# Hybrid encoder layer: the second norm's per-row scale applied behind the MLP, its transposes taken by column half, and the step sizes' sums issued behind the gated attention

## Chip, cores and metric

One core of a Trainium2 chip runs the whole program. Times are device microseconds (us) of that core. Six engines appear below: PE (matrix products, with PEld for its weight loads), DVE, ACT and POOL (elementwise work), SP (issues most DMAs), and the DMA queues.

## What is computed

One encoder layer runs on two requests with the same weights: a prompt of 256 tokens and a sample of 512 tokens, 1024 features each.

```python
def rmsnorm(x, g):
    return x * lax.rsqrt(jnp.mean(x * x, axis=-1, keepdims=True) + EPS) * g

h = rmsnorm(x, norm1)
(gq, gk, gv, gg, glr, dq, dk, dvv, sz, sxbc, sdt) = jnp.split(h @ w_in, IN_OFFSETS, axis=-1)
o_gla  = gla_mixer(gq, gk, gv, gg, glr, ...)     # gated attention, 4 heads, forward and backward
o_diff = diff_mixer(dq, dk, dvv, ...)            # w = softmax 1 - lam * softmax 2, 4 heads
o_ssd  = ssd_mixer(sz, sxbc, sdt, ...)           # state space scan, 8 heads, forward and backward
x = x + jnp.concatenate([o_gla, o_diff, o_ssd], axis=-1) @ w_out
h = rmsnorm(x, norm2)                            # the second norm
x = x + jnp.square(jax.nn.relu(h @ w_mlp1)) @ w_mlp2

# in ssd_mixer: the step sizes and their running sums
dt_f = jax.nn.softplus(sdt[..., :8] + dtb_f)
la   = dt * -exp(alog);  acum = jnp.cumsum(la, axis=1)
```

## The kernel before

**Tiles.** The 768 tokens are six tiles of 128 rows: tiles 0 and 1 are the prompt, tiles 2 to 5 the sample. Every product is made of three passes in a reduced fp32 form, high part by high part and the two mixed ones (mm3, L96 to L100). So each operand is a pair: ACT writes the high part and DVE the rest. Weights go through load_unit (L137): a DMA of 512 KB on SP into wr (two buffers), an ACT cast to wh (L134) and a DVE subtraction to wl (L135). Three kinds of product are used: fm (features on the partitions, 384 token columns in the first projection, 256 or 512 in the MLP), tm (tokens on the partitions, 256 columns), and tp (tokens on the partitions, 512 columns, added to the residual rows xres).

**What sets the order.** The body is written stage after stage, and a framework's scheduler, which has a timing model of its own, merges the stages engine by engine: it takes whatever is ready by that model, earlier-written work and work in a high_priority block first. An engine runs its list strictly in that order, so an instruction that waits holds up all that is behind it on that engine.

**Stages.** First norm and transposes; the first projection's low-rank gate and step-size columns (glr, L234); ssd_dt (L503); gates of the gated attention (gla_gates, L263), whose cores run on DVE, POOL and short products (gla_core, L340); then projections for the other mixers, each interleaved with attention: diff_in (L753) makes queries, keys and values, diff_head (L786) scores sc, softmax pr and its transposed weights wT; SSD convolution and chunks (L566 to L750); then for the prompt W_out (tok_product, L891), second norm (norm2, L1148, which calls norm_transpose, L166) and MLP (mlp, L934), interleaved with the sample's attention and SSD; last the sample's W_out, second norm and MLP, which have no other stage beside them.

**Step sizes (ssd_dt, L503).** On 16 partitions of 768 columns: ACT Abs, Exp, Ln (L507 to L509), then ten DVE instructions with one scan over the tokens (dpre, L522). SP stores rows of the sums to DRAM as scr (L533, L534) and the chunk totals as scp (L535), and reads scp back on all partitions as ptb (L536). ACT makes the decays decs from ptb (L543). PE transposes the sums to tokens on partitions, ACT copies them out of PSUM (tms, L552 to L556) and makes ew from them (L558 to L563). decs, tms and ew are used by the SSD chunks and states.

**Second norm (norm_transpose, L166).** For each row tile: ACT squares and sums a row (L172), DVE makes mean square plus EPS (L158), POOL raises it to -0.5 (L159), DVE writes scaled rows xn (L177). PE transposes xn 128 x 128 into a PSUM tile xT (L184), ACT and DVE apply the feature's gain as they split xT into the pair h (L185, L186). For the sample this runs on two pairs of row tiles, since the last W_out product there goes row tile by row tile (by_tile, L906), and the first MLP block therefore uses two halves of 256 columns. For the prompt it runs once both row tiles are complete.

Of the kernel before, what the change touches and what calls it, by code (L numbers as in the profile page):

```python
# [19 lines left out]
P = 128  # L20
D = 1024
# [21 lines left out]
def hybrid_kernel(ctx, tc, io):  # L43
# [64 lines left out]
    pool.memset(ones, 1.0)  # L108
    nhalf = const.tile([P, 16], F32, name="nhalf")
# [51 lines left out]
    def rstd1(out, ss, scale):  # L161
        rstd_of(out, ss, 1, scale, small2)

    scaled = []

    def norm_transpose(xs, r0, tiles, hT, xn_of, ps_of, small, rstd, c0):  # L166

        xn = []
        for t in tiles:
            y = xn_of(xs[t])  # L170
            ss = small("ss", 1)
            sq = act.activation(y[2], xs[t], AF.Square, accum_out=ss)  # L172
            rs = small("rs", 1)
            rstd(rs, ss, 1.0 / D)
            for i in range(2):
                cs = slice(512 * i, 512 * i + 512)
                scaled[:] = [sq.ins, dve.tensor_scalar(y[i], xs[t][:, cs], rs, None, op0=ALU.mult).ins]  # L177
            xn.append(y)
        n = len(tiles) * P
        sl = slice(c0, c0 + n)  # L180
        for k in range(KT):
            ps = ps_of("xT")
            for i, y in enumerate(xn):
                nc.tensor.transpose(ps[:, i * P:(i + 1) * P], y[k // 4][:, (k % 4) * P:(k % 4 + 1) * P], ident)  # L184
            last = (act.activation(hT[k][0][:, sl], ps[:, :n], AF.Copy, scale=gains[:, r0 + k:r0 + k + 1]),  # L185
                    dve.scalar_tensor_tensor(hT[k][1][:, sl], ps[:, :n], gains[:, r0 + k:r0 + k + 1], rd(hT[k][0][:, sl]),  # L186
                                             op0=ALU.mult, op1=ALU.subtract))
        return last

    hT = [(hs_("hTh", F32R), hs_("hTl", F32R)) for _ in range(KT)]  # L190
    for tiles in ((0,), (1,), (2, 3), (4, 5)):
        normed = norm_transpose(xt, 0, tiles, hT, lambda x: (x[:, 0:512], x[:, 512:1024], junk), mx, small, rstd1, tiles[0] * P)
# [34 lines left out]
    zdt = s3("zdt")  # L227
# [79 lines left out]
    def gla_qk(hp):  # L307
# [195 lines left out]
    def ssd_dt():  # L503

        ps_ = slice(96, 112)
        z, t1, u, l = zdt[ps_], t3("dz")[ps_], t3("dt2")[ps_], t3("dl")[ps_]
# [8 lines left out]
        stk = t3("stk")  # L515
        pool.memset(stk, 0.0)
        dve.scalar_tensor_tensor(stk[0:16], z, 0.0, l, op0=ALU.max, op1=ALU.add)
        dtl = t3("dtl")[ps_]

        dve.tensor_scalar(dtl, stk[0:16], sdtc[0:16, 3:4], -128.0, op0=ALU.mult, op1=ALU.max)  # L520
        inc, exc = t3("dpre")[ps_], t3("dexc")[ps_]
        dve.tensor_tensor_scan(inc, resetm[ps_], dtl, 0.0, ALU.mult, ALU.add)  # L522
# [5 lines left out]
        stb = t3("stb")  # L528
# [6 lines left out]
        nc.sync.dma_start(out=scp, in_=v128(inc)[:, :, 127])  # L535

# [27 lines left out]
        return scr, decs, tms, ew  # L564
# [311 lines left out]


# [13 lines left out]
    def tok_product(op, n, wsrc, k0, tiles, done=None, by_tile=False, after=()):  # L891
# [4 lines left out]
        def product(ps, w, t, i, c):  # L896
            for k in range(4):
                mm3(ps, op(i + k, t), (w[0][:, k], w[1][:, k]), i + k == 0, i + k == n - 1)
            if i + 4 == n:
                cs = slice(c, c + 512)  # L900
                dve.tensor_tensor(xres[t][:, cs], ps, xres[t][:, cs], ALU.add)  # L901
                if done is not None:
                    done(t, c + 512)

        if by_tile:
            ws = [load(c, 0) for c in range(0, D, 512)]  # L906
# [317 lines left out]
```

## Time and profile before

| | us |
|---|---|
| three timed runs | 1166.26, 1168.5, 1172.04 |
| median | 1168.5 |
| the profiled execution | 1169.03 |
| its span in the trace | 1167.2 |
| around the span | 1.83 |

The mean granted clock of TensorE over the span is 0.976 of full speed. Below, the granted clock has two levels: 1.0 in a column PEclk stands for 2.4 GHz and 0.5 for 1.2 GHz. The trace comes from one execution; a group "xT<-ident,xn" means that the instruction writes the tile xT and reads ident and xn. A figure in square brackets is the idle time of the engine ahead of that instruction, with the instruction that ended it.

### The profile page before, as it was taken

The page shows a single profiled execution, that of the slowest core. Times are in us where ns is not written, and L with a number is a line of the kernel's source. Part 1 is how long each engine was busy: PE and PEld are TensorE (multiplying, and loading weights), DVE is VectorE, ACT ScalarE, POOL GpSimd, SP SyncE. Part 2 cuts the span into 40 slices and gives each one's busy share as a digit, 9 for nine tenths or more (in the row PEclk, how much of TensorE's full clock was granted, in tenths as well). Part 3 has the DMA queues.
Part 4 walks back from the last instruction along what each step waited for, and adds up shares of the span by engine and source line. Part 5 has one row for each costly group of instructions (what it writes and reads, how often), then busy time and mean ns, then how long its engine had stood idle before and what let it go on. Part 6 is the DMA issues. An engine that isn't in the chain of part 4 may idle for free.

```text
span 1167.2 us, 19741 instructions
## 1 busy us (share of the span) xinstructions
PE 1110.8 (95%) x7868; PEld 978.6 (84%) x7868; DVE 737.8 (63%) x1298; ACT 563.9 (48%) x1119; POOL 157.0 (13%) x208
## 2 busy tenths in 40 slices
PE   7989797999998999899989999999999999999998
PEld 6989697999998986788877897788887787787786
DVE  6559859563697668887677786846544534434443
ACT  7476666554377237756666573425231332322321
POOL 1002425310401360110100012200000000000000
PEclk9989798899999999899999999999999999999999
DMA  6312021171534355445543549522323323233231
GB/s 196 85 40 74 4 64 38 41 240 39 162 96 127 111 160 167 126 144 177 195 144 120 187 145 305 200 92 73 108 72 108 101 80 108 77 104 99 82 109 72
DMA packets 118642, 136.41 MB, mean 117 GB/s; under 512 B 8936, under 2 KB 86790, under 8 KB 118550
## 3 DMA queue, kind: packets, MB, share of 16 engines
q1 hardware_dynamic: 118517, 135.14, 36.6%
q8 instruction: 62, 1.02, 0.3%
q14 instruction: 31, 0.25, 0.1%
q10 hardware_dynamic: 32, 0.01, 0.0%
HBM read 121.44 MB, written 13.68 MB: 116 GB/s over the span
## 4 chain that ended last, share of the span: by engine, by line
PE 61%; DVE 16%; DMA 11%; ACT 6%; issue 3%; POOL 2%; SPq 0%; DVEq 0%; ACTq 0%; POOLq 0%
PE tp L98 7%; DMA wr<-in_w_mlp 7%; PE tp L99 7%; PE tp L100 7%; PE fm L98 6%; PE fm L100 6%; PE fm L99 6%; PE tm L100 5%; PE tm L99 5%; PE tm L98 5%; DVE wl L135 4%; ACT wh L134 2%; DMA er<-scr 1%; DVE d L428 1%; DVE eq L433 1%
## 5 line engine op out<-in xcount | busy, mean ns | idle before, releaser
L134 ACT CAST wh<-wr 128x1024 fp32r<-128x1024 f32 x186 | 189.2, 1048 | 236.5 <-PE tp L100 129.2
L135 DVE TENSOR_TENSOR wl<-wr,wh 128x1024 fp32r<-128x1024 f32 x186 | 224.2, 1229 | 93.4 <-ACT wh L134 92.8
L100 PE MATMUL tm<-wh,hTl 128*128 128x256 f32 x576 | 168.7, 293 | 0.0
L98 PE MATMUL tm<-wh,hTh 128*128 128x256 f32 x576 | 166.8, 290 | 0.5 <-ACT xp L576 0.5
L99 PE MATMUL tm<-wl,hTh 128*128 128x256 f32 x576 | 166.8, 290 | 0.0
L901 DVE TENSOR_TENSOR xres<-tp,xres 128x512 f32<-128x512 f32 x116 | 77.8, 687 | 100.5 <-PE tp L100 100.3
L99 PEld LDWEIGHTS tm<-wl,hTh 128*128 128x128 f32 x576 | 112.4, 195 | 1.5 <-issue 1.0
L98 PEld LDWEIGHTS tm<-wh,hTh 128*128 128x128 f32 x576 | 112.2, 195 | 1.6 <-ACT xp L576 0.8
L100 PEld LDWEIGHTS tm<-wh,hTl 128*128 128x128 f32 x576 | 112.4, 195 | 0.7 <-issue 0.4
L99 PE MATMUL fm<-h2l,wh 128*128 128x512 f32 (+1 forms) x288 | 107.5, 374 | 0.0
L98 PE MATMUL fm<-h2h,wh 128*128 128x512 f32 (+1 forms) x288 | 107.1, 373 | 0.3 <-ACT h2h L185 0.3
L100 PE MATMUL fm<-h2h,wl 128*128 128x512 f32 (+1 forms) x288 | 107.0, 372 | 0.0
L98 PE MATMUL tp<-wh,uh 128*128 128x512 f32 x256 | 101.7, 397 | 0.6
L99 PE MATMUL tp<-wl,uh 128*128 128x512 f32 x256 | 101.0, 395 | 0.0
L100 PE MATMUL tp<-wh,ul 128*128 128x512 f32 x256 | 99.7, 395 | 0.0
L98 PE MATMUL fm<-h,wh 128*128 128x256 f32 x256 | 72.5, 284 | 3.4 <-ACT relu L947 3.4
L99 PE MATMUL fm<-h,wh 128*128 128x256 f32 x256 | 72.7, 285 | 0.0
L100 PE MATMUL fm<-h,wl 128*128 128x256 f32 x256 | 72.0, 284 | 0.6 <-DVE wl L135 0.6
L947 ACT ACTIVATE relu<-fm 128x256 f32<-128x256 f32 (+1 forms) x68 | 31.7, 469 | 73.2 <-PE fm L100 73.2
L98 PEld LDWEIGHTS fm<-h2h,wh 128*128 128x128 f32 x288 | 54.7, 191 | 10.7 <-ACT h2h L185 0.5
L100 PEld LDWEIGHTS fm<-h2h,wl 128*128 128x128 f32 x288 | 55.0, 191 | 10.1
L99 PEld LDWEIGHTS fm<-h2l,wh 128*128 128x128 f32 x288 | 54.9, 191 | 10.1
(325 smaller groups left out, 2446.7 us busy)
## 6 DMA issues: line engine op xcount, KB each, us to landing
wr<-in_w_mlp SPq DMA_DIRECT2D x128, 512.0 KB
wr<-in_w_in SPq DMA_DIRECT2D x30, 512.0 KB
wr<-in_w_out SPq DMA_DIRECT2D x24, 512.0 KB
ar<-scr SPq DMA_DIRECT2D x6, 512.0 KB
er<-scr SPq DMA_DIRECT2D x6, 512.0 KB
x<-in_x_sample SPq DMA_DIRECT2D x4, 512.0 KB
wr<-in_w_in SPq DMA_DIRECT2D x8, 256.0 KB
xres<-in_x_sample SPq DMA_DIRECT2D x4, 512.0 KB
```

The costliest lines, as they stand in the source:

```text
L98: mm(out, lhsT=lh, rhs=rh, start=first, stop=False)
L99: mm(out, lhsT=lh, rhs=rl, start=False, stop=False)
L100: mm(out, lhsT=ll, rhs=rh, start=False, stop=last)
L134: act.copy(hi, raw)
L135: dve.tensor_tensor(lo, raw, rd(hi), ALU.subtract)
L428: dve.tensor_tensor(D[i].rearrange("p b r i -> p b (r i)"), X.rearrange("p (b i) -> p b i", i=2 * s), bc(ref, [P, nb, 2 * s]), ALU.subtract)
L433: dve.tensor_tensor(parts(eq)[:, :, i], D[i][:, :, i], parts(q)[:, :, i], ALU.mult)
L901: dve.tensor_tensor(xres[t][:, cs], ps, xres[t][:, cs], ALU.add)
L947: act.activation(r, ps, AF.Relu)
```

## The change

**Second norm.** For a constant s > 0, relu(s a)^2 = s^2 relu(a)^2, so a row's factor can leave the MLP as its square. norm2 now transposes the plain rows xres (no xn, no POOL power) and applies the gains as before. scale_of stores 1/(mean square + EPS) of each row (a DVE reciprocal), and the last addition of the MLP becomes one instruction with two operations, product times scale plus xres. Transposes are issued by column half: in the sample as soon as the first 512 columns of all four row tiles are added, four features in a PSUM bank of 512 columns each; in the prompt after the second column half, features 0 to 3 behind tile 0 and 4 to 7 behind tile 1 in program order, two features per bank. The by_tile path is gone, and the first MLP block of the sample uses 512 columns.

**Step sizes.** ssd_dt becomes a generator in three steps: Abs, Exp and Ln stay ahead, behind gla_qk(0); the ten DVE instructions, the scan and the stores to DRAM come after diff_in(0); ptb, decs, tms and ew after diff_in(1). Its tiles come from other buffers. **Copies.** gla_qk's copies out of PSUM become high priority.

```diff
+    def gained(hl, ps, gain):
+        return (act.activation(hl[0], ps, AF.Copy, scale=gain),
+                dve.scalar_tensor_tensor(hl[1], ps, gain, rd(hl[0]), op0=ALU.mult, op1=ALU.subtract))
...
     def keep(dst, scale):
             def consume(ps, ts):
-                act.activation(dst[:, ts], ps, AF.Copy, scale=scale)
+                with tc.high_priority():
+                    act.activation(dst[:, ts], ps, AF.Copy, scale=scale)
...
     def ssd_dt():
-        act.activation(l, t1, AF.Ln, bias=1.0)
+        log_ins.append(act.activation(l, t1, AF.Ln, bias=1.0).ins)
+        yield
+        reset, u = s2("reset")[ps_], i3("dt2")[ps_]
+        resets(reset)
         dve.tensor_scalar(u, t1, 1.0, -1.0, op0=ALU.add, op1=ALU.add)
...
-        dve.tensor_tensor_scan(inc, resetm[ps_], dtl, 0.0, ALU.mult, ALU.add)
+        dve.tensor_tensor_scan(inc, reset, dtl, 0.0, ALU.mult, ALU.add)
...
         nc.sync.dma_start(out=scp, in_=v128(inc)[:, :, 127])
+        yield
         ptb = const.tile([P, 2, 8, NT], F32, name="ptb")
...
-        return scr, decs, tms, ew
+        yield scr, decs, tms, ew
...
+                    if scales is None:
+                        added[t] = dve.tensor_tensor(xres[t][:, cs], sums[t], xres[t][:, cs], ALU.add).ins
+                    else:
+                        dve.scalar_tensor_tensor(xres[t][:, cs], sums[t], scales[t], xres[t][:, cs], op0=ALU.mult, op1=ALU.add)
...
-    dt = ssd_dt()
     pre = [gla_gates(hp) for hp in range(2)]
...
     qk = gla_qk(0)
+    dt_steps = ssd_dt()
+    next(dt_steps)
     core = gla_core(pre[0], qk, v)
...
     for p in range(2):
         diff_in(p)
+        dt = next(dt_steps)
         take_turns(*(diff_head(p, h, 0) for h in range(2)))
...
-    def xn_of(x):
-        a, b = dn("xn"), dn("xn")
-        return a, b, a.bitcast(mybir.dt.bfloat16)
-
-    def norm2(tiles, h2, c0, ps_of):
-        return norm_transpose(xres, 8, tiles, h2, xn_of, ps_of, small2, rstd1, c0)
+    def scale_of(t):
+        ss, ms = small2("ss", 1), small2("ms", 1)
+        act.activation(dn("sq").bitcast(mybir.dt.bfloat16), xres[t], AF.Square, accum_out=ss)
+        dve.tensor_scalar(ms, ss, 1.0 / D, EPS, op0=ALU.mult, op1=ALU.add)
+        scales[t] = scale[:, t:t + 1]
+        dve.reciprocal(scales[t], ms)
+
+    def norm2(tiles, ks, h2, ps_of):
+        n = len(tiles) * P
+        per = 512 // n
+        for k0 in range(ks.start, ks.stop, per):
+            ps = ps_of("xT")
+            for k in range(k0, k0 + per):
+                pk = ps[:, (k - k0) * n:(k - k0) * n + n]
+                for i, t in enumerate(tiles):
+                    nc.tensor.transpose(pk[:, i * P:(i + 1) * P], xres[t][:, k * P:(k + 1) * P], ident)
+                normed[:] = [z.ins for z in gained(h2[k], pk, gains[:, 8 + k:9 + k])]
...
+    def prompt_done(t, c):
+        if c == D:
+            norm2(prompt, range(4 * t, 4 * t + 4), h2p, acc)
+            scale_of(t)
+    tok_product(y_op, 4, w_out, 8, prompt, prompt_done)
...
+    def sample_done(t, c):
+        if t == 5:
+            norm2(sample, range(c // P - 4, c // P), h2s, mx)
+        if c == D:
+            scale_of(t)
+    tok_product(y_op, 4, w_out, 8, sample, sample_done)
     for f in range(0, 4096, 512):
-        mlp(f, 512, [(h2s, 0, 256, 0), (h2s, 256, 256, 256)] if f == 0 else [(h2s, 0, 512, 0)], sample, pair_of(i3), dn,
-            store if f == 4096 - 512 else None)
+        mlp(f, 512, [(h2s, 0, 512, 0)], sample, pair_of(i3), dn, store if f == 4096 - 512 else None)
```

**How the instructions move.** In the fences for the kernel now, L numbers are lines of the changed file. Behind the glr products, 165 of the 384-column products stood on PE ahead of the first gate product, and 90 stand there now; between the first gate product and the first product of the gated attention stood 75 of them and 162 of the 256-column tm products, now 150 and 89. From the first to the last product of the first gated core, PE has 102 tm products where it had 83, and of the second 96 where it had 79.

ACT around the wait for ptb, before: the sums' copies stk, two weight casts, one key copy, then decs, which reads ptb, and behind it the PSUM copies tms.

```order
L313 ACTIVATE gk_821<-fm_886 128x384
L524 COPY stk_662<-dpre_667 16x768
L525 COPY stk_662<-dexc_668 16x768
L134 CAST wh_1700<-wr_1702 128x1024
L134 CAST wh_1700<-wr_1706 128x1024
L313 ACTIVATE gk_821<-fm_912 128x384
L543 ACTIVATE decs<-ptb 64x48 x2
L552 COPY tms<-tms_688 128x4x16
```

ACT around the same wait now, in the prompt's attention: dqk and dsq are the next queries' copies out of PSUM and their squares, wt the copy of transposed softmax weights, pr the exponentials of the scores.

```order
L527 COPY stk_3478<-dpre_3482 16x768
L528 COPY stk_3478<-dexc_3483 16x768
L765 COPY dqk_3751<-tm_3702 128x512
L767 ACTIVATE dsq_3753<-dqk_3751 128x512
L765 COPY dqk_3816<-tm_3767 128x512
L767 ACTIVATE dsq_3818<-dqk_3816 128x512
L547 ACTIVATE decs<-ptb 64x48 x2
L852 CAST wt_3554<-wT_3572 128x2x128
L765 COPY dqk_3881<-tm_3832 128x512
L135 CAST wh_4102<-wr_4104 128x1024
L135 CAST wh_4102<-wr_4108 128x1024
L842 ACTIVATE pr_3581,dsum_3578<-sc_3584,dmx_3582 128x256
```

decs moved from a place with the tms copies behind it to one with the copies and exponentials of the prompt's attention behind it.

PE at the prompt's second norm, before: after the W_out products come two score products of the sample's attention, then the transposes of xn, then the transposes of softmax weights (wT).

```order
L836 MATMUL sc_5700<-kz_2946,qs_5569 128x512
L184 MATMUL xT_7026<-ident,xn_7006 128x128
L184 MATMUL xT_7031<-ident,xn_7006 128x128
L184 MATMUL xT_7036<-ident,xn_7006 128x128
L184 MATMUL xT_7026<-ident,xn_7016 128x128
L184 MATMUL xT_7031<-ident,xn_7016 128x128
L184 MATMUL xT_7036<-ident,xn_7016 128x128
L184 MATMUL xT_7041<-ident,xn_7006 128x128
L184 MATMUL xT_7041<-ident,xn_7016 128x128
L184 MATMUL xT_7046<-ident,xn_7007 128x128
```

The same place now:

```order
L840 MATMUL sc_5703<-kz_2884,qs_5572 128x512
L1166 MATMUL xT_7033<-ident,xres_6751 128x128
L1166 MATMUL xT_7033<-ident,xres_6753 128x128
L1166 MATMUL xT_6995<-ident,xres_6751 128x128
L1166 MATMUL xT_6995<-ident,xres_6753 128x128
L1166 MATMUL xT_7042<-ident,xres_6751 128x128
L1166 MATMUL xT_7042<-ident,xres_6753 128x128
L1166 MATMUL xT_7004<-ident,xres_6751 128x128
L1166 MATMUL xT_7004<-ident,xres_6753 128x128
L848 MATMUL wT_5711<-ident,pr_5695 128x128 x4
L839 MATMUL sc_5729<-ks_5608,qs_5607 128x512
```

Eight transposes of plain rows stand in one row ahead of wT, where twelve of xn did.

PE at the sample's second norm, before: transposes of the last pair of tiles' xn stand between products fm of the first MLP block, 256 columns each.

```order
L100 MATMUL tp_9329<-wh_9161,mol_9147 128x512
L184 MATMUL xT_9272<-ident,xn_9228 128x128
L184 MATMUL xT_9272<-ident,xn_9238 128x128
L184 MATMUL xT_9277<-ident,xn_9228 128x128
L184 MATMUL xT_9277<-ident,xn_9238 128x128
L98 MATMUL fm_9415<-h2h_9111,wh_9403 128x256
L99 MATMUL fm_9415<-h2l_9112,wh_9403 128x256
L184 MATMUL xT_9282<-ident,xn_9228 128x128
```

The same place now:

```order
L100 MATMUL tp_9306<-wh_9236,mol_9138 128x512
L1166 MATMUL xT_9320<-ident,xres_8773 128x128
L1166 MATMUL xT_9320<-ident,xres_8775 128x128
L1166 MATMUL xT_9327<-ident,xres_8773 128x128
L1166 MATMUL xT_9327<-ident,xres_8775 128x128
L98 MATMUL fm_9366<-h2h_9102,wh_9354 128x512
L99 MATMUL fm_9366<-h2l_9103,wh_9354 128x512
L100 MATMUL fm_9366<-h2h_9102,wl_9355 128x512
L1166 MATMUL xT_9320<-ident,xres_8777 128x128
```

The products of the first block read features 0 to 3 (h2 9102 onwards), whose transposes ended a column half earlier, while the transposes of the second half stand between them.

## Rows read from the trace of the kernel before

**Rows 1.** The page's first part, busy time and share of the span by engine, and the shares of the chain that ended last.

```profile
PE 1110.8 (95%) x7868; PEld 978.6 (84%) x7868; DVE 737.8 (63%) x1298; ACT 563.9 (48%) x1119; POOL 157.0 (13%) x208
...
PE 61%; DVE 16%; DMA 11%; ACT 6%; issue 3%; POOL 2%; SPq 0%; DVEq 0%; ACTq 0%; POOLq 0%
```

**Rows 2.** Busy time by engine in the stretch around the gates' start, from the table by stretches. Columns: stretch, its length, PE busy (instructions), PEld, DVE, ACT, POOL, then granted clock PEclk, DMA share, GB/s.

```profile
70.20:77.00 6.80, 5.09 (x16) 4.90 (x17) 0.34 (x2) 6.17 (x24) 0.00 (x0) 0.50 0.40 140
77.00:80.00 3.00, 3.00 (x19) 2.96 (x18) 1.34 (x2) 3.00 (x7) 0.00 (x0) 1.00 0.00 0
```

**Rows 3.** The chain that ended last, around ptb: start, length, who.

```profile
57.57 1.76 DVE dpre L522
59.35 0.31 SPq L533
59.71 6.74 DMA scp<-dpre
66.51 4.25 DMA ptb<-scp
```

**Rows 4.** The timeline of ACT and PE at the end of that chain: start, length, engine, line, operation, shapes, and in brackets the idle time before.

```profile
70.78 0.58 ACT L543 ACTIVATE decs<-ptb 64x48 f32<-64x48 f32 x2 [7.20 <-DMA ptb<-scp]
...
71.91 0.80 PE L274 MATMUL gate<-rst,wg 96*128 96x512 f32 x1 [3.73 <-ACT tms L552]
```

**Rows 5.** Two stretches of the gated attention's cores, columns as in rows 2.

```profile
128.20:138.40 10.20, 6.86 (x316) 6.19 (x315) 10.20 (x19) 4.03 (x8) 3.64 (x2) 1.00 0.02 5
...
196.50:206.70 10.20, 6.49 (x209) 6.34 (x210) 10.10 (x15) 5.25 (x11) 6.39 (x4) 0.50 0.01 4
```

**Rows 6.** The timeline of PE in a full row of tm products, the first and the last of a row with 16 intervals between their starts.

```profile
272.43 0.28 PE L98 MATMUL tm<-wh,hTh 128*128 128x256 f32 x1
...
274.30 0.28 PE L99 MATMUL tm<-wl,hTh 128*128 128x256 f32 x1
```

**Rows 7.** The timeline of DVE in the step sizes: three of the ten instructions; the scan is in rows 3, and the other six take 0.95 or 0.96 each, as the last one here.

```profile
51.14 0.56 DVE L510 TENSOR_SCALAR dt<-dz 16x768 f32<-16x768 f32 x1 [0.52 <-ACT dz L508]
...
56.92 0.61 DVE L520 TENSOR_SCALAR dtl<-stk,sdtc 16x768 f32<-16x768 f32 x1
...
59.36 0.95 DVE L523 TENSOR_TENSOR dexc<-dpre,dtl 16x768 f32<-16x768 f32 x1
```

**Rows 8.** The prompt's attention with the projections beside it, two stretches that follow each other, columns as in rows 2.

```profile
220.00:260.00 40.00, 40.00 (x345) 40.00 (x344) 24.93 (x72) 22.05 (x57) 13.34 (x7) 1.00 0.50 152
260.00:375.00 115.00, 112.19 (x797) 110.72 (x796) 78.97 (x180) 64.96 (x147) 15.54 (x30) 0.99 0.38 116
```

**Rows 9.** The timeline of ACT and DVE in one turn of the prompt's attention, from the copies of the next queries to the scaled weights pr.

```profile
273.68 0.59 ACT L761 COPY dqk<-tm 128x512 f32<-128x512 f32 x1 [2.63 <-PE tm L100]
274.16 2.00 ACT L134 CAST wh<-wr 128x1024 fp32r<-128x1024 f32 x2
...
276.59 0.36 ACT L848 CAST wt<-wT 128x256 fp32r<-128x256 f32 x1
276.85 0.48 ACT L838 ACTIVATE pr<-sc,dmx 128x256 f32<-128x256 f32 x1
...
278.79 0.48 DVE L841 SCALAR_TENSOR_TENSOR pr<-pr,dratio 128x256 f32<-128x256 f32 x1
```

**Rows 10.** The prompt's second norm: two stretches, columns as in rows 2.

```profile
462.30:469.50 7.20, 3.71 (x23) 2.06 (x22) 6.92 (x17) 6.20 (x13) 2.68 (x6) 1.00 0.00 0
469.50:476.40 6.90, 3.90 (x14) 3.04 (x15) 6.41 (x13) 2.85 (x8) 1.25 (x1) 0.51 0.48 152
```

**Rows 11.** The timeline of PE there.

```profile
468.76 0.52 PE L184 MATMUL xT<-ident,xn 128*128 128x128 f32 x3 [2.85 <-DVE xn L177]
...
472.35 1.54 PE L184 MATMUL xT<-ident,xn 128*128 128x128 f32 x6 [3.06 <-DVE h L186]
```

**Rows 12.** The timeline of DVE there.

```profile
465.89 1.28 DVE L837 TENSOR_REDUCE dmx<-sc 128x1 f32<-128x512 f32 x2
...
467.15 0.41 DVE L660 TENSOR_TENSOR st<-st,decs 128x256 f32<-128x256 f32 x1
...
469.08 2.76 DVE L135 TENSOR_TENSOR wl<-wr,wh 128x1024 fp32r<-128x1024 f32 x2
...
471.83 1.24 DVE L186 SCALAR_TENSOR_TENSOR h<-xT,gains,h 128x256 fp32r<-128x256 f32 x3
...
473.23 0.75 DVE L841 SCALAR_TENSOR_TENSOR pr<-pr,dratio 128x512 f32<-128x512 f32 x1
```

**Rows 13.** The sample's second norm on PE, the timeline.

```profile
798.44 0.30 PE L184 MATMUL xT<-ident,xn 128*128 128x128 f32 x1 [0.33 <-DVE h2l L186]
...
802.30 0.74 PE L184 MATMUL xT<-ident,xn 128*128 128x128 f32 x5 [1.92 <-DVE xn L177]
...
803.32 0.51 PE L98 MATMUL fm<-h2h,wh 128*128 128x256 f32 x2 [0.29 <-ACT h2h L185]
```

**Rows 14.** The stretch behind it, and the sample's MLP, columns as in rows 2.

```profile
804.00:807.40 3.40, 3.40 (x18) 3.40 (x17) 2.51 (x7) 1.02 (x4) 0.00 (x0) 0.51 0.75 243
...
820.00:1167.00 347.00, 342.78 (x1489) 275.34 (x1488) 151.39 (x184) 92.96 (x120) 0.00 (x0) 1.00 0.29 93
```

**Rows 15.** The costliest groups by line, shapes kept apart: busy us, mean ns of one, idle time ahead.

```profile
L901 DVE TENSOR_TENSOR xres<-tp,xres 128x512 f32<-128x512 f32 x116 | 77.8, 687 | 100.5 <-PE tp L100 100.3
...
L186 DVE SCALAR_TENSOR_TENSOR h2l<-xT,gains,h2h 128x256 fp32r<-128x256 f32 x16 | 7.0, 478 | 2.9 <-ACT h2h L185 2.9
```

More of the change, by code (lines that the diff above doesn't have):

```diff
@@ L108, in hybrid_kernel @@
     pool.memset(ones, 1.0)
+    scale = const.tile([P, NT], F32, name="scale")
     nhalf = const.tile([P, 16], F32, name="nhalf")
@@ L191, in hybrid_kernel @@
     for tiles in ((0,), (1,), (2, 3), (4, 5)):
-        normed = norm_transpose(xt, 0, tiles, hT, lambda x: (x[:, 0:512], x[:, 512:1024], junk), mx, small, rstd1, tiles[0] * P)
+        normed = norm_transpose(tiles)
     log_ins = []
@@ L226, in hybrid_kernel @@
     rst = s3("rst", F32R)
-    zdt = s3("zdt")
+    zdt = i3("zdt")
     def glr_consume(ps, ts):
@@ L889, in mix_operands, with tok_product @@
         return res
-    def tok_product(op, n, wsrc, k0, tiles, done=None, by_tile=False, after=()):
+    def tok_product(op, n, wsrc, k0, tiles, done=None, after=(), scales=None):
         def load(c, i):
             return load_unit(lambda r: [(0, 512, wsrc[:, k0 + i + r.start:k0 + i + r.stop, c:c + 512])], (4, 512))
[L896 to L906, printed above, removed]
-            for t in tiles:
-                for c in range(0, D, 512):
-                    product(acc("tp"), ws[c // 512], t, 0, c)
-            return
         for c in range(0, D, 512):
-            sums = {}
+            sums, cs = {}, slice(c, c + 512)
             for i in range(0, n, 4):
@@ L920, in tok_product @@
                         sums[t] = acc("tp")
-                    product(sums[t], w, t, i, c)
+                    for k in range(4):
+                        mm3(sums[t], op(i + k, t), (w[0][:, k], w[1][:, k]), i + k == 0, i + k == n - 1)
+                    if i + 4 < n:
+                        continue
+                    if scales is None:
+                        added[t] = dve.tensor_tensor(xres[t][:, cs], sums[t], xres[t][:, cs], ALU.add).ins
+                    else:
+                        dve.scalar_tensor_tensor(xres[t][:, cs], sums[t], scales[t], xres[t][:, cs], op0=ALU.mult, op1=ALU.add)
+                    if done is not None:
+                        done(t, c + 512)
     def from_column(ops, c0):
@@ L955, in mlp @@
                 u.append((uh, ul))
-        tok_product(from_column(u, tiles[0]), n // P, w2, f // P, tiles, done, after=last)
+        tok_product(from_column(u, tiles[0]), n // P, w2, f // P, tiles, done, last, scales)
     def pair_of(new):
@@ L1163, in hybrid_kernel @@
     tok_product(from_column(mix_operands(mixa[0], range(4), u_new, dn), 0), 4, w_out, 4, prompt)
-    tok_product(y_op, 4, w_out, 8, prompt)
     h2p = [both_in(hp_)("h2", 256) for _ in range(KT)]
-    normed = [z.ins for z in norm2(prompt, h2p, 0, acc)]
+    def prompt_done(t, c):
[3 more added lines that the diff above has]
+    tok_product(y_op, 4, w_out, 8, prompt, prompt_done)
     for f in range(0, 4096, N_F):
-        mlp(f, N_F, [(h2p, 0, 256, 0)], prompt, u_new, dn, store if f == 4096 - N_F else None, (scaled, normed) if f == 0 else ())
+        mlp(f, N_F, [(h2p, 0, 256, 0)], prompt, u_new, dn, store if f == 4096 - N_F else None,
+            ([added[t] for t in prompt], list(normed)) if f == 0 else ())
     for t in sample:
```

50 lines of the change are left out of this document (22 added, 28 removed).

## Prediction

> **What bounds the kernel now.** I read the page's shares first. PE is busy 95% of the span and holds 61% of the chain that ended last, with DVE at 16% and DMA at 11% [rows 1]. So a change gains only where PE stands idle or at its lower clock, and an instruction removed from DVE, ACT or POOL gains nothing unless PE waits for it. Next I read the tables by stretches for the places where PE's busy time falls short of the stretch or the granted clock is 0.5. Four of them bear on this change: the start of the gates [rows 2], the gated attention's cores [rows 5], the prompt's second norm [rows 10] and the sample's [rows 13, 14]. Where the change moves work to, in the prompt's attention, PE is full today [rows 8].
>
> The sum is made against the profiled execution, 1169.03, which is 0.5 above the median of the three runs, well inside their spread. About 0.5%, 5.8 us, is what a measurement can tell from no change here, so faster begins at 1163.2.
>
> **Term 1, the wait ahead of the gates goes: -6.3.** The chain shows it whole: the scan, an issue on SP, scp to DRAM in 6.74 us, ptb back in 4.25 [rows 3]. ACT then stands 7.20 us at decs, and the PSUM copies tms are queued behind it, so PE idles 3.73 us at the first gate product [rows 4]. Over the 6.80 us from 70.2 PE is busy 5.09 at half clock, and full clock is back from 77.0 [rows 2]; at full clock the same work is 2.55. That gives 3.73 + 2.55 = 6.3. With decs and tms gone from that place, the gates need only their own operands, which are ready, and free PSUM banks, which the copies with high priority now give. Bounds: -3.7 (the clock falls anyway) and -6.3.
>
> **Term 2, more cover in the gated attention: -4.2.** In both cores DVE is the full engine (10.20 of 10.20, 10.10 of 10.20) and PE is busy 6.86 and 6.49 there [rows 5], so a product moved into such a stretch costs nothing where it came from and fills idle time. By the order the first core has 102 tm products beside it where it had 83, the second 96 where it had 79: 36 more. One tm product of 256 columns takes (274.30 - 272.43)/16 = 0.117 us of PE at full clock [rows 6]. 36 x 0.117 = 4.2. Bounds: 0, if these products fall where PE was already covered, and -5 (the clock in the second core, 0.50 in rows 5, rises a little too).
>
> **Term 3, the wait for ptb in its new place: +6.** The chain behind the scan is the same: 70.76 - 59.33 = 11.4 us from the scan's end to ptb's landing [rows 3]. By the order the scan now stands behind the last maximum of the first pair's scores; with a maximum at 0.6, dtl at 0.61 and the scan at 1.75 [rows 12, 7, 3] it ends some 3 us after the last score product, and ptb lands at 14.4. Behind decs on ACT stand wt (0.36), dqk (0.59), two casts (2.00), then the two exponentials (0.48 and about 0.2 for each sum read out), and on DVE the scaling of pr, 0.48 [rows 9]. With decs' 0.58 [rows 4] and DVE's small steps this is about 5.5 us, so the second pair's transposes wT can start at about 20. Until then PE has 130 tm products, 130 x 0.117 = 15.2, and its scores, some 0.5: it idles about 4.3. A fall of the clock follows an idle stretch of this length in rows 2 and rows 10, where 3.9 to 5.1 us of work ran at half clock and cost half of that, 2.0 to 2.5; I take 1.7, since the idle time lies next to a full row. Together +6. Bounds: 0, if ptb lands 5 us sooner; +10, if the two stores of the sums and the reads of scr, which are now issued around ptb on SP, put 4 us more on it.
>
> **Term 4, the ten DVE instructions beside the prompt's attention: +1.** They are 0.56 + 0.61 + 1.75 + 7 x 0.95 = 9.6 us [rows 7, 3]. Today they hide before the gates. In the new place DVE is busy 24.93 of 40 and 78.97 of 115 us [rows 8], so the room is there, and the tm products ahead of them cover most. What remains is a delay of one row maximum. Bounds 0 and +9.6 (every one of them ahead of what PE waits for).
>
> **Term 5, the prompt's second norm: 0.** Today PE idles 2.85 for xn and 3.06 for a PSUM tile to be emptied by DVE (h) [rows 11], at half clock afterwards, 3.90 of 6.90 busy [rows 10]. xn goes from the path. But DVE was full there (6.92 of 7.20, 6.41 of 6.90) [rows 10], and PE's next instruction after the eight transposes is wT, which waits for DVE's pr. Between the last addition and that pr DVE still has two wl (2.76), two maxima (1.28), three h (1.24), three st (3 x 0.41), pr (0.75) [rows 12] and about 0.7 of single-column steps: 8.0. PE's work in this time is eight transposes at 0.52/3 [rows 11] and two scores, about 2. So it idles about 6, as 2.85 + 3.06 = 5.9 do now, and the wait for xn gives way to one for pr. Bounds: -4 (the casts come later, and 2.76 falls out) and +4 (a second wait at the wT after it, which has some 2 us of products before it).
>
> **Term 6, the sample's second norm: -4.2.** The waits 0.33 + 1.92 + 0.29 = 2.5 go [rows 13]: features 0 to 3 are transposed a column half early, and the first products of the MLP need only those. In their place the second half's transposes wait for the last additions, 0.69 each [rows 15], while PE has 15 products of 0.233 (347.00/1489) [rows 14] between them. The 3.40 us at half clock after it [rows 14] become 1.7. 192 products of 0.117 become 96 of 0.233: equal. 2.5 + 1.7 = 4.2. Bounds: -2 (clock) and -6 (the evictions of 256, 0.48 each on DVE [rows 15], held more than the rows show).
>
> **Edits at nothing.** 80 final additions take a second operand instead of none: on DVE the plain addition is 0.69, the two-operation form of 256 columns 0.48 [rows 15], so I see at most 0.3 more each; in the sample's MLP DVE is busy 151.39 of 347.00 [rows 14], and only the last of them stands on the end: 0 to +0.3. POOL's powers go; nobody waited for them alone. The rows of ACT's square and DVE's reciprocal have the whole MLP to finish. The scheduler's other shifts in order: 0, with 5 either way.
>
> Sum: -6.3 - 4.2 + 6 + 1 + 0 - 4.2 = -7.7, so 1161.3.
>
> **Rival 1, the transfers are quicker in the new place.** scp's 6.74 and ptb's 4.25 [rows 3] are of a few KB; should both take as long as the shorter, the chain is 8.9, wT could start at 17.5 against 15.7 of cover, and term 3 is 1.8 without a fall of the clock: 1157. Against it speaks that both were measured while weights moved, as they do in the new place (DMA share 0.50 and 0.38 [rows 8]). The Trainium skill, page "DMA: Bandwidth & Descriptors", section "Latency and other measured facts", gives about 2 us as a DMA's fixed cost; by that rule the two would be 4 us, an estimate, the wait would be covered whole, term 3 would be 0 and the time 1155.3. This case's trace disagrees with it at 6.74 and 4.25 [rows 3], and the sum goes by the trace.
>
> **Rival 2, no difference to be told.** The reads of scr, issued ahead of ptb, hold it back by 2 us (term 3 at +8), DVE's step sizes delay two maxima (term 4 at +2), and the cores take only half of the new cover, because there the products come in a bunch (term 2 at -2): -6.3 - 2 + 8 + 2 + 0 - 4.2 = -2.5, so 1166.5. For it speaks that terms 2 and 3 both rest on the order and on durations from elsewhere.
>
> **Rival 3, slower.** The step sizes stand in DVE's list ahead of the maxima and scalings on which the prompt's softmax depends. Softmax has one chain, scores, maximum, exponentials, scaling, transposes, and PE's cover for a turn is 15.2 us. If the chain with ptb in it is longer than that by all of the 9.6, that is if DVE's instructions and the wait add up and don't overlap, terms 3 and 4 are +10 and +9.6, term 2 is -2: -6.3 - 2 + 10 + 9.6 - 4.2 = +7.1, so 1176. It decides from the point where the DVE work delays the scan's own end past the 3 us assumed. Against it: DVE has a third of those stretches free [rows 8].
>
> That the change doesn't do what it says I put at 1%: the order shows decs gone from ahead of the gates and xres in the transposes.
>
> **Numbers.** Forecast 1161.3, chance 0.46, own range 1156 to 1167 (term 3 from 2 to 10, term 5 either way). Rival 1 has 0.17, rival 2 0.26, rival 3 0.10. Of the forecast's 0.46 some 0.10 lies above 1163.2, so faster is 0.36 + 0.17 = 0.53, same 0.10 + 0.26 = 0.36 with the rest, slower 0.11. The range from 1152 to 1172 leaves out most of rival 3 and the far end of rival 1.
>
> **What would show it.** Term 1: no idle time at the first gate product, clock 1.0 through that stretch. Term 2: PE busier than 6.9 of 10.2 beside a full DVE. Term 3: ACT idle at decs, released by ptb, and then PE idle at a wT of the prompt; none there means rival 1. Term 5: PE idle at wT for pr behind the eight transposes. Term 6: no idle of over 0.5 us between tp and the first block's products. The forecast is wrong if PE's idle time at the prompt's wT is over 10 us, or if a new wait appears at the W_out products for a weight or a PSUM bank.

## The result and the profile after

The changed kernel is slower: 1182.32 us median of four runs (1180.89 to 1187.65) against 1168.33 (1166.26 to 1172.04); ratio 1.0118, 95% interval 1.0088 to 1.0148. The profiled execution took 1183.39 us, with a span of 1181.6. The forecast was 1161.3 and its range ended at 1172.

The page of the changed kernel, first part and the chain's shares, beside [rows 1]:

```profile
PE 1109.5 (94%) x7772; PEld 973.3 (82%) x7772; DVE 743.5 (63%) x1276; ACT 561.1 (47%) x1103; POOL 154.3 (13%) x204
...
PE 67%; DVE 13%; DMA 9%; ACT 5%; issue 3%; POOL 2%; SPq 0%; ACTq 0%; DVEq 0%; POOLq 0%
```

Shares say nothing about where 14 us went: PE's busy time even fell by 1.3. So I cut both traces at instructions that both have (first gate product, first and last product of the gated cores, first scores, first xtmp, first transpose of the second norm, first product of the prompt's MLP, of the sample's W_out from its moh operands, of its MLP). In each stretch I add up, over PE's products, the time from one start to the next less what its columns take at full clock (0.117 us per 256 columns [rows 6]; 0.056 to 0.07 for short products). The sum holds idle time and half clock alike. The totals differ by 15.0 between the kernels and the spans by 14.4, so the cut accounts for the difference to 0.6. Each column is one execution: the changed kernel and e3, whose order on PE is the same, differ by 4.0 in the prompt's MLP, so a difference of a few us in one line is not told from chance by one column alone.

| lost on PE, us | before | after | norm only e1 | sums only e2 | decs pinned e3 | earlier e4 | earlier, sums only e6 | sample's norm e9 | prompt's norm e12 | e14 |
|---|---|---|---|---|---|---|---|---|---|---|
| to the first gate | 9.4 | 11.0 | 12.6 | 9.1 | 12.3 | 12.1 | 9.0 | 9.1 | 11.3 | 9.2 |
| to the gated cores | 8.5 | 2.1 | 8.0 | 1.9 | 2.5 | 2.1 | 1.9 | 8.8 | 7.7 | 2.3 |
| gated cores | 41.5 | 40.1 | 42.4 | 37.6 | 40.6 | 43.5 | 40.5 | 41.4 | 42.8 | 41.0 |
| to the first scores | 1.3 | 1.5 | 1.4 | 1.5 | 1.5 | 9.0 | 8.5 | 1.7 | 1.4 | 5.0 |
| to the first xtmp | 2.7 | 19.9 | 3.0 | 19.7 | 12.3 | 3.4 | 2.7 | 3.3 | 2.9 | 7.6 |
| to the prompt's norm | 18.5 | 17.3 | 17.4 | 21.9 | 22.0 | 19.9 | 18.7 | 19.0 | 17.1 | 15.4 |
| prompt's norm | 9.2 | 8.9 | 6.3 | 8.7 | 7.8 | 7.8 | 8.6 | 9.7 | 6.3 | 9.8 |
| prompt's MLP | 28.3 | 36.2 | 23.6 | 28.2 | 32.2 | 32.7 | 30.5 | 28.8 | 25.6 | 26.2 |
| sample's W_out | 3.4 | 6.5 | 17.5 | 5.5 | 5.8 | 5.8 | 4.4 | 4.3 | 11.0 | 4.7 |
| sample's norm and MLP | 9.8 | 4.2 | 4.1 | 8.8 | 4.2 | 4.2 | 8.0 | 5.2 | 10.7 | 4.7 |

The first line is hardly chance. The norm part also rewrote the first norm's function, and with it the row factor rs of the first norm comes from another pool of small tiles (small2 in place of small), which the section on the change does not show. In the table the five kernels without that line lose 9.0 to 9.4, the five with it (the changed kernel, e1, e3, e4, e12) 11.0 to 12.6. Of the other six, e10 and e13 without it lose about 9, e7 and e11 with it 11.3 and 13.4, and e8 and e5, one of each, meet at about 10.4. The table by stretches, before and after, columns as in [rows 2]:

```profile
10.00:20.00 10.00, 9.12 (x58) 8.52 (x58) 9.43 (x31) 9.70 (x26) 2.57 (x5) 1.00 0.78 240
...
10.00:20.00 10.00, 8.13 (x43) 6.82 (x43) 8.93 (x28) 8.44 (x23) 2.34 (x5) 1.00 0.83 251
```

By the order, that one line is enough: put into the kernel before by itself, it gives every engine the order that e12 has up to the second norm. It was not run by itself.

The changed kernel gains 6.4 ahead of the cores and 5.6 at the end, as forecast. It loses 1.6 at the first norm, 17.2 between the first scores and xtmp, and 7.9 and 3.1 behind the prompt's norm.

The large one first. The chain that ended last, of the changed kernel, answers to [rows 3]:

```profile
260.36 1.77 DVE dpre L525
...
262.49 6.78 DMA scp<-dpre
269.33 5.97 DMA ptb<-scp
...
275.62 0.28 ACT decs L547
```

The timeline of ACT and PE there, and at xtmp; columns as in [rows 4]:

```profile
275.33 0.58 ACT L547 ACTIVATE decs<-ptb 64x48 f32<-64x48 f32 x2 [8.69 <-DMA ptb<-scp]
...
281.15 0.69 PE L848 MATMUL wT<-ident,pr 128*128 128x128 f32 x2 [7.21 <-DVE pr L845]
...
358.60 1.54 PE L602 MATMUL xtmp<-ident,zh 128*128 128x128 f32 x6 [5.44 <-DVE zh L598]
```

The table by stretches of the changed kernel; columns as in [rows 2]:

```profile
253.00:273.90 20.90, 20.90 (x179) 20.74 (x177) 12.62 (x20) 8.27 (x17) 0.00 (x0) 1.00 0.33 65
273.90:278.30 4.40, 0.04 (x1) 0.00 (x0) 0.83 (x2) 2.91 (x6) 0.00 (x0) 1.00 0.48 123
278.30:285.20 6.90, 4.05 (x19) 4.05 (x20) 4.68 (x11) 4.55 (x13) 0.00 (x0) 0.51 0.53 152
...
356.80:363.70 6.90, 5.10 (x18) 5.10 (x19) 6.11 (x9) 3.05 (x5) 0.00 (x0) 0.51 0.55 154
```

PE runs full until 273.90, then has nothing: ACT stands at decs, and behind it in ACT's list are the copy wt and the exponentials of the next scores. The idle time is 7.21. From 278.30, still inside it, the granted clock is 0.51 for 6.90 us, in which 4.05 us of PE's work stand. The same pair comes again at xtmp, 5.44 of idle time and 6.90 at half clock that begin inside it. There the wait ends with DVE's zh, and DVE works without a pause, but no more so than in the same 20 us of the kernel before (first line):

```profile
329.30:349.30 20.00, 19.78 (x119) 19.22 (x118) 19.54 (x35) 13.89 (x29) 0.00 (x0) 1.00 0.29 86
...
338.60:358.60 20.00, 14.56 (x86) 14.21 (x85) 19.74 (x32) 14.33 (x32) 0.17 (x3) 0.96 0.28 72
```

What differs is DVE's order. Now two weights' low parts wl, 2.36 us, stand ahead of the zh that xtmp waits for; before, the next wl stood behind it. Now, then before:

```profile
354.99 2.36 DVE L136 TENSOR_TENSOR wl<-wr,wh 128x1024 fp32r<-128x1024 f32 x2
...
357.59 0.95 DVE L598 SCALAR_TENSOR_TENSOR zh<-xp,zh 128x772 f32<-128x772 f32 x1
...
348.29 0.96 DVE L594 SCALAR_TENSOR_TENSOR zh<-xp,zh 128x772 f32<-128x772 f32 x1
...
349.83 1.22 DVE L135 TENSOR_TENSOR wl<-wr,wh 128x1024 fp32r<-128x1024 f32 x1
```

At the second norms, the timeline of PE, beside [rows 11] and [rows 13]:

```profile
478.78 0.44 PE L1166 MATMUL xT<-ident,xres 128*128 128x128 f32 x2 [1.74 <-DVE h L165]
480.76 1.14 PE L1166 MATMUL xT<-ident,xres 128*128 128x128 f32 x4 [1.54 <-DVE h L165]
482.92 1.12 PE L848 MATMUL wT<-ident,pr 128*128 128x128 f32 x4 [1.01 <-DVE pr L845]
...
802.88 1.04 PE L1166 MATMUL xT<-ident,xres 128*128 128x128 f32 x8
804.45 0.60 PE L1166 MATMUL xT<-ident,xres 128*128 128x128 f32 x4
807.68 0.60 PE L1166 MATMUL xT<-ident,xres 128*128 128x128 f32 x4
```

In the sample PE no longer waits for a transpose; in the prompt three waits of 4.3 together stand where 5.9 did. A wait that the prediction named as a sign of being wrong, for a weight at a W_out product, is there as well, the sample's first one:

```profile
739.43 0.80 PE L98 MATMUL tp<-wh,moh 128*128 128x512 f32 x1 [2.52 <-ACT wh L135]
```

### The profile page after: what moved, and what is told of

The parts are those of the page before. It is cut to its first block, busy times and chain, and to the rows that moved or that the text cites. A ratio compares the mean times of both kernels' runs of the same rounds, so it can differ in the third digit from the quotient of the medians.

```text
span 1181.6 us, 19519 instructions
## 1 busy us (share of the span) xinstructions
PE 1109.5 (94%) x7772; PEld 973.3 (82%) x7772; DVE 743.5 (63%) x1276; ACT 561.1 (47%) x1103; POOL 154.3 (13%) x204
## 4 chain that ended last, share of the span: by engine, by line
PE 67%; DVE 13%; DMA 9%; ACT 5%; issue 3%; POOL 2%; SPq 0%; ACTq 0%; DVEq 0%; POOLq 0%
PE fm L98 8%; PE fm L99 8%; PE fm L100 8%; PE tp L98 8%; PE tp L99 8%; PE tp L100 7%; DMA wr<-in_w_mlp 6%; PE tm L98 5%; PE tm L99 5%; PE tm L100 5%; DVE wl L136 4%; ACT wh L135 2%; DVE eq L432 1%; DVE d L427 1%; POOL wx L653 1%
## 5 line engine op out<-in xcount | busy, mean ns | idle before, releaser
L136 DVE TENSOR_TENSOR wl<-wr,wh 128x1024 fp32r<-128x1024 f32 x186 | 226.8, 1244 | 98.3 <-ACT wh L135 96.6
L919 DVE SCALAR_TENSOR_TENSOR xres<-tp,scale,xres 128x512 f32<-128x512 f32 x80 | 58.2, 747 | 79.7 <-PE tp L100 79.7
L100 PE MATMUL fm<-h2h,wl 128*128 128x512 f32 x256 | 101.1, 395 | 0.0
L98 PE MATMUL fm<-h2h,wh 128*128 128x512 f32 x256 | 100.9, 396 | 0.0
L99 PE MATMUL fm<-h2l,wh 128*128 128x512 f32 x256 | 100.8, 394 | 0.0
L98 PEld LDWEIGHTS tp<-wh,uh 128*128 128x128 f32 x256 | 48.0, 188 | 15.4 <-DVE xres L919 4.6
L952 DVE TENSOR_TENSOR relu<-relu 128x512 f32<-128x512 f32 x32 | 22.0, 690 | 59.9 <-ACT relu L948 59.9
L100 PEld LDWEIGHTS tp<-wh,ul 128*128 128x128 f32 x256 | 48.2, 188 | 11.5
```

The lines of the kernel that those rows point to most:

```text
L98: mm(out, lhsT=lh, rhs=rh, start=first, stop=False)
L99: mm(out, lhsT=lh, rhs=rl, start=False, stop=False)
L100: mm(out, lhsT=ll, rhs=rh, start=False, stop=last)
L136: dve.tensor_tensor(lo, raw, rd(hi), ALU.subtract)
L919: dve.scalar_tensor_tensor(xres[t][:, cs], sums[t], scales[t], xres[t][:, cs], op0=ALU.mult, op1=ALU.add)
L952: dve.tensor_tensor(r, r, r, ALU.mult)
```

## Experiments

Each time is the median in its job, with the ratio to the kernel before in the same job and the 95% interval.

**e1 and e2, the parts by themselves.** e1 takes the norm part of the diff, e2 the rest. Against the changed kernel, e1 has

```diff
+    dt = ssd_dt()
     pre = [gla_gates(hp) for hp in range(2)]
...
-    dt_steps = ssd_dt()
-    next(dt_steps)
```

and e2

```diff
-    tok_product(y_op, 4, w_out, 8, prompt, prompt_done)
+    tok_product(y_op, 4, w_out, 8, prompt)
+    normed = [z.ins for z in norm2(prompt, h2p, 0, acc)]
```

> The norm part of the change alone; step sizes and their sums as before. Theory A (each part costs in the places where its instructions stand): the sample's second norm gives about 5 us as in the changed kernel, the prompt's MLP with the sample's attention beside it loses about 8 and the sample's W_out about 3, so about 1174, the wait of 3.7 us at the first gate product still there. Theory B (what was lost behind the prompt's attention comes from the step sizes' move): 1163, the MLP stretch as before.

> The move of the step sizes' sums alone; second norm as before. Theory A: the gates give 5 us, the prompt's attention loses 17 (7 us idle at a transpose wT behind decs' wait for ptb, some 5 at a transpose of the convolution, and half clock behind each), so about 1180. Theory B: the losses in the prompt's MLP come with it too, about 1187.

e1: 1172.48, 1.0031 (1.0009 to 1.0054). e2: 1178.71, 1.0066 (1.0041 to 1.0090). The two add to 0.97% of the 1.18%. e2 holds the whole loss at the attention (19.7), nothing of it is in e1: theory A. e1 is slower by less than A's 6 us, and its loss sits elsewhere than in the changed kernel: the first norm loses 3.2, the prompt's MLP gains 4.7 and the sample's W_out loses 14.1. By the table 2.9 of e1's 3.7 us lie ahead of the second norm and go with rs's pool, so the second norm's own part comes out near nothing, and a place can't be pinned on it. High priority for gla_qk's copies, which e2 also has, alone leaves every engine's order as it was, so it was not run.

**e3, the wait for ptb alone.** PE's, SP's and POOL's orders stay.

```diff
+            with tc.issue_after(last copy of the attention's values, dv):
                 act.activation(decs[gs], ptb[...], AF.Exp)
```

> The changed kernel with decs alone issued later on ACT, behind the last copy of the attention's values; PE's, SP's and POOL's order are those of the changed kernel. Theory A: the wait for ptb costs 7 us of idle time and 3.4 us of half clock, both go: about 1172. Rival: the softmax chain is held up by the ten step-size instructions on DVE as well, so PE idles at the same transpose for 3 us or more: 1177 to 1182.

1176.88, 1.0055 (1.0033 to 1.0077): about 7 us of the 14 come back. The wait at wT is gone and the stretch loses 12.3 instead of 19.9. What stays is xtmp:

```profile
353.22 1.54 PE L603 MATMUL xtmp<-ident,zh 128*128 128x128 f32 x6 [5.64 <-DVE zh L599]
```

The wait for ptb is shown as one cause. The time misses A's 1172 in part because A put half clock at 3.4 where 2.0 were lost; the rival's idle time at wT isn't there, and the stall at xtmp was in the changed kernel already.

**e4 and e6, the ten DVE instructions elsewhere.** The sums go ahead of diff_in(0), with decs pinned as in e3; e4 on the changed kernel, e6 with the second norm as before.

```diff
+    next(dt_steps)
     for p in range(2):
         diff_in(p)
-        dt = next(dt_steps)
+        if p == 1:
+            dt = next(dt_steps)
```

> The changed kernel with decs issued behind the last copy of the attention's values (as in e3) and the ten step-size instructions and the stores ahead of the first projection of the attention, behind the gated attention, where DVE is least busy. Theory A: those 9.6 us on DVE (with the decay rows ar that follow them) are what makes DVE late at the convolution's transposes xtmp, 5.6 us idle in e3 and half clock behind; the stall goes and the time falls from e3's 1176.9 to about 1168. Rival: DVE is late there because of how the convolution's own instructions now stand together; the stall stays, about 1177.

> The kernel before with the step sizes' sums at the earlier place of e4 and decs behind the last copy of the attention's values; second norm as before. Theory A: the gates' 5 us remain gained and neither wait comes in its place: about 1163. Rival (some wait always takes the place of the one removed, since an order that the scheduler makes anew costs as much): 1169 or more.

e4: 1176.3, 1.0058 (1.0036 to 1.0080). e6: 1169.06, 0.9984 (0.9964 to 1.0004). The loss ahead of xtmp falls to 3.4 and 2.7, as theory A says. But its reason isn't shown. The decay rows ar stay in that stretch in both, 2.8 us of DVE. And in e3, DVE is busy only 27.02 of the 49 us behind the scan, so it has time to work off 9.6 us; columns as in [rows 2]:

```profile
266.00:315.00 49.00, 47.36 (x379) 46.80 (x378) 27.02 (x76) 25.90 (x66) 9.89 (x10) 0.97 0.36 96
```

What e4 and e6 also change is DVE's order: no wl stands in its list in the last 5 us ahead of xtmp. Over all kernels of this study the stall goes with that. In the six that have two wl there (the changed kernel, e2, e3, e5, e13, e14) PE idles 3.56 to 5.71 at xtmp, in the ten others 0.12 at most. In e13 and e14 the ten instructions end over 20 us ahead of the first scores, and the stall is there; e14:

```profile
348.17 1.22 DVE L136 TENSOR_TENSOR wl<-wr,wh 128x1024 fp32r<-128x1024 f32 x1
349.30 0.96 DVE L608 SCALAR_TENSOR_TENSOR zh<-xp,zh 128x772 f32<-128x772 f32 x1
...
350.31 1.25 PE L612 MATMUL xtmp<-ident,zh 128*128 128x128 f32 x6 [3.58 <-DVE zh L608]
```

With all ten on DVE in the stretch the idle time is 5.44 to 5.71, without them 3.58 and 4.02: the ten may be worth some 2 us of it. No run moves the two wl alone, so the rest is put down to them by what goes together, not by an experiment. In e4 and e6 the total hardly moves against e3 and the kernel before, because a new wait stands where the sums now are, 9.0 and 8.5 in the table. PE in e6:

```profile
215.88 0.58 PE L98 MATMUL tm<-wh,hTh 128*128 128x256 f32 x1 [5.34 <-ACT dqk L773]
```

PE waits for ACT's copy of the queries out of PSUM, and that copy is queued behind the twelve squares of the gated output and the copies stk of the sums.

**e5, the same instructions on POOL.** Seven of the ten go from DVE to POOL, in e3's place, such as

```diff
-        dve.tensor_tensor(exc, inc, dtl, ALU.subtract)
+        pool.tensor_tensor(exc, inc, dtl, ALU.subtract)
```

> As e3, with seven of the ten step-size instructions on POOL in place of DVE. Theory A: DVE's time is what counts, 6.6 us of it go, so the idle time at xtmp falls from 5.6 to 1 us or less: about 1170. Rival, the order: no less than 4 us of idle time there, 1175 to 1178.

1174.64, 1.0040 (1.0023 to 1.0056). The idle time at xtmp falls from 5.64 to 3.56, and a new one of 3.04 comes at wT. Neither expectation held, and the order changed with it, so it is inconclusive by itself.

**e7, the sample by row tile.** As e1, but by_tile again, with plain rows and the scale behind the MLP.

```diff
-        if t == 5:
-            norm2(sample, range(c // P - 4, c // P), h2s, mx)
+        if t % 2 and c == D:
+            norm2((t - 1, t), range(KT), their columns of h2s, mx)
```

> The norm part alone, as e1, but the sample's last W_out product again row tile by row tile, transposes behind each pair of tiles, first MLP block in halves. Theory A: going by column half makes the product need the SSD outputs of all four row tiles in its first half, which come late through DRAM (waits of 5.2 and 2.4 us for moh in e1); by tile these fall to about 1 us each, and some 2.5 us of waits at the second norm come back: about 1167. Rival: the waits for moh come from the order in which the SSD's chunks now end and stay: 1172 to 1175.

1171.88, 1.0018 (0.9996 to 1.0040), no different from e1. W_out loses 10.1 instead of 17.5, and the norm and MLP 8.5 instead of 4.1. So going by column half accounts for 7.4 at W_out and gives back 4.4 behind it; 6.7 of W_out's loss stay by tile as well, and the time is at the rival's edge.

**e8, the sums inside the first projection; e9, the sample's half of the norm part; e10, both; e11, e8's place in the changed kernel.** In e9, the orders up to the sample's last W_out product are those of the kernel before. The edits of e8 and e9:

```diff
             tm_unit(w, cons)
+            if p == 0 and i == 0:
+                next(dt_steps)
...
-    tok_product(y_op, 4, w_out, 8, sample, lambda t, c: norm2(...), True)
+    tok_product(y_op, 4, w_out, 8, sample, sample_done)
```

> The kernel before with the step sizes' sums behind the first pair's query projection, that is inside the attention's first projection, and decs behind the last copy of the attention's values; second norm as before. In e6 the wait of 5.3 us at a tm product is put down to ACT's queue, where the two copies stk (1.7 us) and the gated attention's twelve squares stand ahead of the copy of the queries. Theory A: behind the queries the copies come after it, the wait goes, and what is left is the gain at the gates: about 1163. Rival: the twelve squares alone keep the copy waiting, or the DVE work comes late again at xtmp: 1168 or more.

> The kernel before with the sample's second norm alone changed: plain rows transposed by column half, scale behind the MLP, last W_out product by column, first MLP block of 512 columns; the prompt's norm as before. Up to the sample's last W_out product every engine has the order of the kernel before. Theory A (the norm part's own gain is at the sample, and what e1 lost came from a new order of the prompt's MLP and the sample's attention): idle time at the sample's norm falls by 5 us, nothing else changes, 1163 to 1165. Rival: the product by column half waits for the last row tiles' operands whatever the order ahead of it, 3 to 8 us as in e1: 1167 to 1172.

> e8 and e9 together: the sums behind the first pair's queries, decs pinned, and the sample's second norm alone changed. Theory A: the two gains stand in different places and add up, about 1158. Rival: what is gained early is taken back by waits for weights later, 1163 or more.

> The changed kernel with the sums behind the first pair's queries and decs pinned: as e8, but with the whole norm part, prompt and sample. Theory A: about 5 us under e4, 1170, so still above e10 by what the prompt's half of the norm part costs in the prompt's MLP (8 to 12 us). Rival: the norm part costs nothing by itself, 1160.

e8: 1172.79, 1.0021 (0.9999 to 1.0042). e9: 1166.4, 0.9970 (0.9955 to 0.9985). e10: 1166.53, 0.9973 (0.9953 to 0.9993). e11: 1172.92, 1.0031 (1.0013 to 1.0049). e9 is theory A: the sample's half gains 4.6 at its place, and no other stretch is more than 0.9 worse. e10 is its rival: e8's loss ahead of the scores, 11 us, is in it too. e11 gives back 0.87% of the changed kernel's 1.18%, and is still 0.6% above e10, which lacks the prompt's half and rs's other pool; in their traces e11 loses 8.7 more from the prompt's norm on, and 4.7 more at the first norm. e8's time is the rival's, for a reason that neither theory gave. In its trace the scan holds up ACT's list, SP's as well:

```profile
229.54 0.83 ACT L532 COPY stk<-dpre 16x768 f32<-16x768 f32 x1 [4.05 <-DVE dpre L530]
231.26 0.83 ACT L533 COPY stk<-dexc 16x768 f32<-16x768 f32 x1 [0.90 <-DVE dexc L531]
232.10 0.59 ACT L773 COPY dqk<-tm 128x512 f32<-128x512 f32 x1
...
229.47 0.29 SPq L541 DMA_DIRECT2D scr<-dpre  x1
```

PE waits 3.33 for that dqk, and 2.32 later for a transfer of the queries that SP issued behind the stores.

**e12, the prompt's half alone.** Against e1, the sample's part is the one of the kernel before:

```diff
-    tok_product(y_op, 4, w_out, 8, sample, sample_done)
+    tok_product(y_op, 4, w_out, 8, sample, lambda t, c: scaled rows xn, transposed by pair, True)
```

> The kernel before with the prompt's second norm alone changed; the sample's norm, its last product by row tile and its first MLP block in halves as before. Theory A: e1 is 0.3% slower with both halves and e9 0.3% faster with the sample's half, so the prompt's half alone costs 0.6%: about 1176, the loss between the start of the prompt's MLP and the sample's norm. Rival: the two halves only cost together, the product by column half waiting for operands that the new order brings late: 1168 to 1170.

1174.65, 1.0035 (1.0017 to 1.0053). The prompt's half costs by itself, less than the 0.6% expected. By the table e12 loses 4.2, of which 1.3 ahead of the second norm, where its order differs from the kernel before by rs's pool alone. Behind it 2.9 are gained at the norm and 2.7 in the MLP, and 7.6 lost in the sample's W_out. There ACT stands 11.61 for the sums' rows er, and moh, the W_out operand, is behind it; PE waits 2.85 for it, the longest wait of that stretch:

```profile
743.01 2.44 ACT L669 ACTIVATE er<-er,tms 128x128 f32<-128x128 f32 x8 [11.61 <-DMA er<-scr]
745.37 0.60 ACT L135 CAST moh<-mo 128x512 fp32r<-128x512 f32 x1
...
746.02 0.51 PE L98 MATMUL tp<-wh,moh 128*128 128x512 f32 x1 [2.85 <-ACT moh L135]
```

By the order, 1080 MLP products stand ahead of the last scores of the sample, where 984 did: the MLP runs out earlier, and the end of the SSD, a chain of short steps and transfers, has only W_out beside it (234 of its products ahead of the SSD's last transpose, 132 before). In the changed kernel these counts are 947 and 129, so this is e12's reason (and e1's), not the changed kernel's. The edit also pins the first MLP weights behind other instructions than before (the last additions in place of the scaled rows xn); no run parts that from the transposes.

**e13 and e14, nothing at the head of a queue that waits for the scan.** As e8, with the copies stk on ACT behind the last dv of the first pair and scr and scp on SP behind its last store; e14 adds e9.

```diff
+        with tc.issue_after(last dv copy of pair 0):
+            act.copy(stk[32:48], inc)
+            act.copy(stk[64:80], exc)
...
+        with tc.issue_after(last store of dv of pair 0):
             nc.sync.dma_start(out=scr[0:8, :], in_=inc[0:8])
```

> As e8, but ACT's copies stk are issued behind the last copy of the first pair's values, and the stores of the sums behind the last store of these values on SP, so nothing that waits for the scan stands ahead of the projection's copies, stores or weights; decs pinned as before; second norm as before. Theory A: each price of e6 and e8 (5.3 us at a tm product; 3.3 us there and 2.3 at the transposes of the queries) came from an instruction that waits for the scan at the head of a queue, and goes: about 1163. Rival: some other wait of the same size takes the place, 1168 or more.

> e13 and the sample's half of the norm part (e9) together. Theory A: both gains, about 1159. Rival: as e10, 1166.

e13: 1165.91, 0.9961 (0.9941 to 0.9981). e14: 1162.34, 0.9931 (0.9908 to 0.9954), faster than both kernels. Theory A, short by a few us: e14 still loses 5.0 and 7.6 around the scores, where the kernel before loses 1.3 and 2.7, the second at xtmp as shown above.

## Why the prediction was wrong

The sign was wrong. What failed is term 4, by 7 us, and the zero for "other shifts in order", by 11 behind the prompt's norm and 1.6 at the first norm. Both priced the move by the instructions named in the change and took every engine's order around them to cost nothing. Terms 2 and 3 were mis-sized by some 3 us each.

- **Term 1 (-6.3): right.** The stretch ahead of the cores went from 8.5 to 2.1, in every kernel without decs there.
- **Term 2 (-4.2): too large.** 41.5 became 40.1; the kernels with the sums moved have 37.6 to 43.5. More products beside a full DVE did not reliably fill it.
- **Term 3 (+6): right mechanism, too small.** The chain took 275.33 - 262.13 = 13.2 where I had 11.4, idle time was 7.21 where I had 4.3, and half clock cost half of 4.05, 2.0, where I had 1.7: 9.2, close to my upper bound of 10. e3 gives back 7.6 of it. The Trainium skill, page "DMA: Bandwidth & Descriptors", section "Latency and other measured facts", gives a fixed cost of about 2 us for a DMA; this trace disagrees again, at 6.78 and 5.97. Where I wrote "a few KB" for both, scp is 0.4 KB and ptb 48 KB.
- **Term 4 (+1): the failed step.** I argued that "the room is there" from DVE's share over 115 us, and looked for no more than the delay of one row maximum. The room lies ahead of the convolution; in the last 20 us ahead of xtmp DVE works without a pause, before and after, and there its order counts. 5.44 of idle time and half of 5.10 by the clock were lost there, 8.0 where I had 1. The loss goes with two wl ahead of the last zh, in e13 and e14 also without the ten instructions in the stretch; these seem to be worth some 2 us of the idle time. How they make the rest, if they do, is open. Rival 3, with a chance of 0.10, had DVE late by the ten instructions' own 9.6 us and at the softmax; e3's trace has no such wait.
- **Term 5 (0): right in sum, not in kind.** 9.2 became 8.9; but PE waits 1.74 and 1.54 for PSUM tiles and only 1.01 for pr, where I had 6 for pr.
- **Term 6 (-4.2): right.** 9.8 became 4.2, and e9 measures -0.30%, 3.5 us.
- **Other shifts (0, with 5 either way): wrong by 11, and by 1.6 at the first norm.** The prompt's MLP and the sample's W_out lost 7.9 and 3.1; in e3, with the same order on PE, 3.9 and 2.4. That it comes with the prompt's half of the norm part is shown by e9 against e12 (1.4 and 4.9 lost there) and by e10 against e11 (1.0 and 10.6). In e12 the longest piece is a wait for late SSD rows. In the changed kernel it is spread over small waits for weights and half clock in the prompt's MLP, and what made these is open.

## What to carry to other kernels

Free time on an engine is to be read in the stretch just ahead of the instruction that will wait, not as an average over the stage, and so is the order of its list there: two instructions that had stood behind the awaited one went with a stall of 3.6 us and more. Before a step that waits for a DMA or a scan is moved, look at what stands behind it in each queue that it uses, SP's included, at the new place; pinning only the copies and stores that wait for the scan behind their neighbours turned +0.21% (e8) into -0.39% (e13). Split a change that has a local and a reordering half: the sample's half alone kept its gain, the prompt's half lost more behind the norm than it gained there. And compare whole kernels, not the edits that are meant to count: a buffer of the first norm, taken from another pool, went with 1.6 to 3.2 us more loss there in the five kernels of the table that had it.

## What was not expected

scp (0.4 KB) and ptb (48 KB) took 6.78 and 5.97 us beside a DMA share of 0.33 (0.48 at ptb's end), as long as in the kernel before (6.74) and longer (4.25). An idle stretch of 5.44 on PE cost another 2.55 by the clock alone: 5.10 us of work ran in the 6.90 us at half clock.
